# Loading the first tile by partitions instead of by tokens in a weighted combine of expert outputs

## The chip, the cores and the metric

The kernel runs on one core of one Trainium2 chip. The metric is the device time of one execution in microseconds (us); lower is better. Most executions of a kernel agree within 0.3%.

## The reference

For every one of 16 x 1024 = 16,384 tokens there are k = 2 expert outputs of 512 float32 numbers each and two weights. The result is the weighted sum of the two.

```python
batch, seq, hidden, n_experts, k = 16, 1024, 512, 8, 2
expert_outputs: [batch, seq, k, hidden] float32      # 67.1 MB
combine_weights: [batch, seq, k] float32

weights = combine_weights[..., np.newaxis]
return np.sum(expert_outputs * weights, axis=2).astype(np.float32)   # 33.6 MB
```

## The kernel before

Each of the 128 partitions of the on-chip memory takes 128 tokens. A token is one row of 4 KB in the input (two experts of 2 KB) and 2 KB in the output. The tokens of one partition lie one behind the other in HBM, so that a partition's part of a load is one contiguous run: 13 tokens are 52 KB. (The last 13 tokens of every partition come from a second region of the input, which changes nothing in this.)

The work is cut into ten tiles of 12 or 13 tokens per partition, all 128 partitions wide (`TILES`). One tensor `et` holds four rooms, `ROOM = [13, 13, 12, 13]`, and tile g uses room g mod 4. Per tile:

- A load from HBM into the room, issued by SyncE (`load`, line 76). Loads go to SyncE's DMA queue, called q1 in the profile.
- `combine`: for tiles 0 to 7, one VectorE multiplication of the whole room with the broadcast weights (line 88) and one VectorE addition of the two halves (line 97), which writes the sums densely into the front of the room. Tile 8 is shared between ScalarE (line 92) and VectorE (lines 94, 96, 97). Tile 9 goes token by token, ScalarE (line 102) and then VectorE (line 103).
- A store from the room to the output (line 130). Stores of tiles 0 to 6 are issued by ScalarE into its own DMA queue, called q10; tiles 7 and 8 together, and tile 9, are stored by SyncE.

After the store of tile g is issued, SyncE is given the load of tile g + 4, which has to wait until that store has landed, since it overwrites the same room.

The order is written out by hand. Before the loop over tiles, ScalarE's queue takes a small store of zeros (`zt`, 16 rows of 512 B), the weights `wt` of the first 115 tokens of each partition (115 KB, `weights`, line 79) and the remaining weights in two small pieces. SyncE's queue takes the loads of tiles 0 to 3. Tile 0 is loaded in two pieces, 2 tokens and then 11 tokens, the first of them with packets limited to 4 KB. The first multiplication on VectorE needs both pieces and the weights.

A DMA is dealt out over up to 16 DMA engines; each row of a load is one packet on one of them, unless a limit on the packet size cuts it. Both queues are served by the same 16 engines.

Of the kernel before, what the change touches and what calls it, by code (L numbers as in the profile page):

```python
# [1 line left out]

# [4 lines left out]


@with_exitstack
def kernel(  # L10
    ctx: ExitStack,
    tc: tile.TileContext,
    expert_outputs: bass.AP,
    combine_weights: bass.AP,
    out: bass.AP,
):

    nc = tc.nc
    b, s, k, h = expert_outputs.shape
    assert k == 2
    n = b * s
    P = nc.NUM_PARTITIONS
    per = n // P
    assert per * P == n

    ROOM = [13, 13, 12, 13]
    ROOMS = len(ROOM)  # L30
    SITE = [sum(ROOM[:i]) for i in range(ROOMS)]
    TILES = [13, 13, 12, 13, 13, 13, 12, 13, 13, 13]
    FIRST = [2, 11, 13, 12, 13]
    STORES = [[0], [1], [2], [3], [4], [5], [6], [7, 8], [9]]
    WHOLE = [0, 1, 2, 3, 4, 5, 6, 7]
    MIXED = [8]
    ALONE = 3
    FREE = {9: 0}
    LAST = 13
    assert all(c <= ROOM[g % ROOMS] for g, c in enumerate(TILES))  # L40
    assert sum(TILES) == per and [g for st in STORES for g in st] == list(range(len(TILES)))
    main = per - LAST
    starts = [sum(TILES[:g]) for g in range(len(TILES))]

    def rows(x):

        first = x[0 : P * main, :].rearrange("(p t) f -> p t f", p=P)
        second = x[P * main : n, :].rearrange("(p t) f -> p t f", p=P)
        return lambda t, c: first[:, t : t + c, :] if t < main else second[:, t - main : t - main + c, :]

    flat = out.rearrange("b s h -> (b s) h")
    eo = rows(expert_outputs.rearrange("b s k h -> (b s) (k h)"))
    cw = rows(combine_weights.rearrange("b s k -> (b s) k"))
    o = rows(flat)

    dt = mybir.dt.float32
    mult = mybir.AluOpType.mult
    add = mybir.AluOpType.add
    copy = mybir.ActivationFunctionType.Copy

    pool = ctx.enter_context(tc.tile_pool(name="all", bufs=1))
    et = pool.tile([P, sum(ROOM), k * h], dt)
    halves = et.rearrange("p j (k h) -> p (j k) h", k=k)
    wt = pool.tile([P, per * k], dt)
    wk = wt.rearrange("p (t k) -> p t k", k=k)
    zt = pool.tile([16, 128], dt)
    warm = pool.tile([P, 1], dt)

    def place(t):
        g = max(g for g in range(len(TILES)) if starts[g] <= t)  # L70
        return SITE[g % ROOMS] + t - starts[g]

    def load(t, c, **kw):
        at = place(t)
        assert place(t + c - 1) == at + c - 1
        nc.sync.dma_start(out=et[:, at : at + c], in_=eo(t, c), **kw)  # L76

    def weights(q, t, c):
        q.dma_start(out=wk[:, t : t + c, :], in_=cw(t, c))

    def combine(g, base):
        at, c, t0 = SITE[g % ROOMS], TILES[g], starts[g]
        if g in WHOLE or g in MIXED:
            room = halves[:, k * at : k * (at + c), :]
            x0, x1 = et[:, at : at + c, 0:h], et[:, at : at + c, h : 2 * h]
            if g in WHOLE:
                wb = wt[:, k * t0 : k * (t0 + c)].unsqueeze(2).to_broadcast([P, k * c, h])
                nc.vector.tensor_tensor(out=room, in0=room, in1=wb, op=mult)  # L88
            else:
                for i in range(ALONE, c):  # L90
                    x = et[:, at + i, 0:h]
                    nc.scalar.activation(out=x, in_=x, func=copy, scale=wt[:, k * (t0 + i) : k * (t0 + i) + 1])  # L92
                w1 = wk[:, t0 : t0 + c, 1:2].to_broadcast([P, c, h])
                nc.vector.tensor_tensor(out=x1, in0=x1, in1=w1, op=mult)  # L94
                w0 = wk[:, t0 : t0 + ALONE, 0:1].to_broadcast([P, ALONE, h])
                nc.vector.tensor_tensor(out=x0[:, 0:ALONE], in0=x0[:, 0:ALONE], in1=w0, op=mult)  # L96
            nc.vector.tensor_tensor(out=halves[:, base : base + c, :], in0=x0, in1=x1, op=add)  # L97
            return
        for i in range(c):
            t = k * (t0 + i)  # L100
            x0, x1 = halves[:, k * (at + i), :], halves[:, k * (at + i) + 1, :]
            nc.scalar.activation(out=x0, in_=x0, func=copy, scale=wt[:, t : t + 1])  # L102
            nc.vector.scalar_tensor_tensor(  # L103
                out=halves[:, base + i, :], in0=x1, scalar=wt[:, t + 1 : t + 2], in1=x0, op0=mult, op1=add
            )

    with tc.manual_schedule():
        nc.vector.memset(zt, 0.0)  # L108

        ahead = flat[0 : P * main, :].rearrange("(q t) h -> q (t h)", q=16)  # L110
        nc.scalar.dma_start(out=ahead[:, 0:128], in_=zt)  # L111
        weights(nc.scalar, 0, main)
        for half in (slice(0, P // 2), slice(P // 2, P)):
            nc.scalar.dma_start(out=wk[half, main:per, :], in_=cw(main, per - main)[half])
        nc.scalar.activation(out=warm, in_=nc.const_aps.tensor(1.0, (P, 1), dt), func=copy)  # L115

        t = 0
        for i, c in enumerate(FIRST):
            load(t, c, **({"max_dma_last_dim": k * h * 4} if i == 0 else {}))
            t += c  # L120
        assert t == sum(TILES[:ROOMS])
        for j, st in enumerate(STORES):
            room = FREE.get(st[0], st[0] % ROOMS)
            base, c = SITE[room] * k, 0
            for g in st:
                combine(g, base + c)
                c += TILES[g]
            assert c <= k * ROOM[room]
            q = nc.sync if j in (7, 8) else nc.scalar
            q.dma_start(out=o(starts[st[0]], c), in_=halves[:, base : base + c, :])  # L130
            for g in st:
                if g + ROOMS < len(TILES):
                    load(starts[g + ROOMS], TILES[g + ROOMS])


# [1 line left out]
_INS = ['expert_outputs', 'combine_weights']  # L137
_OUTS = [((16, 1024, 512), 'float32')]


# [23 lines left out]
```

## Time and profile before

| What | Value |
|---|---|
| Median time of 3 runs | 238.85 us (238.83 to 238.9) |
| The profiled execution: span, first to last instruction | 237.1 us |
| The profiled execution's own time (taken as the median of the runs, since no other time of it is given) | 238.85 us, so some 1.75 us lie outside the span |
| VectorE (DVE) busy | 190.0 us, 80% of the span |
| ScalarE (ACT) busy | 15.8 us, 7% |
| HBM read, written | 67.24 MB, 33.56 MB |
| Mean rate of all DMA | 425 GB/s |
| Share of the 16 DMA engines: queue q1, queue q10 | 75.9%, 23.0% |

In the profile, DVE is VectorE, ACT is ScalarE, SP is SyncE; "SPq" and "ACTq" are the instruction queues of SyncE and ScalarE, where DMAs are issued and semaphores waited for. L88 is line 88 of the kernel. `et<-in_expert_outputs_dram` is a load, `out_dram<-et` a store. The row of digits after DMA gives the busy share of the DMA engines in 40 equal slices of the span, in tenths, 9 being 90% or more. A row of windows gives the stretch, its length, the busy time of each engine with the number of its instructions, the clock, the DMA share and the rate. DMA packets include completion marks of 4 B, one for each engine that takes part in a DMA. A packet is counted in the stretch in which it starts.

### The profile page before, as it was taken

How to read it: one execution, taken by the hardware profiler on the slowest of the kernel's cores; microseconds unless marked ns; L12 is line 12 of the kernel's file. 1: busy time of each engine (PE TensorE's matmuls, PEld its weight loads, DVE VectorE, ACT ScalarE, POOL GpSimd, SP SyncE). 2: the span in 40 equal slices, each digit the busy share in tenths (PEclk: the TensorE clock that was granted, in tenths of full speed). 3: DMA queues.
4: the chain of work that ended last, by engine and by line, in shares of the span. 5: the costliest groups of instructions: out<-in, count | busy, mean ns of one | idle time of the engine just before them, and what ended most of it. 6: DMA issues, size and time to landing. Idle time of an engine off the chain costs nothing.

```text
span 237.1 us, 154 instructions
## 1 busy us (share of the span) xinstructions
DVE 190.0 (80%) x33; ACT 15.8 (7%) x25; POOL 0.2 (0%) x4
## 2 busy tenths in 40 slices
DVE  0006999999999999999999998998499969919400
ACT  2000000000000000000000000000000055019200
POOL 0000000000000000000000000000000000000000
DMA  8999999989999999999899999999899999899996
GB/s 300 388 481 434 432 421 398 470 348 485 449 431 458 431 440 390 486 420 420 359 492 409 409 509 392 431 503 431 359 431 503 420 397 483 381 431 431 431 431 287
DMA packets 3344, 100.80 MB, mean 425 GB/s; under 512 B 512, under 2 KB 656, under 8 KB 912
## 3 DMA queue, kind: packets, MB, share of 16 engines
q1 hardware_dynamic: 2000, 77.33, 75.9%
q10 hardware_dynamic: 1344, 23.47, 23.0%
HBM read 67.24 MB, written 33.56 MB: 425 GB/s over the span
## 4 chain that ended last, share of the span: by engine, by line
DVE 55%; DMA 36%; issue 1%; ACT 0%; DVEq 0%; ACTq 0%; SPq 0%
DVE et L88 35%; DVE et L97 17%; DMA out_dram<-et 17%; DMA et<-in_expert_outputs_dram 12%; DMA wt<-in_combine_weights_dram 8%; DVE et L103 3%; ACT et L102 0%; DVEq L159 0%; ACTq L111 0%; DVE zt L108 0%; DVEq L88 0%; SPq L76 0%; ACTq L102 0%
## 5 line engine op out<-in xcount | busy, mean ns | idle before, releaser
L88 DVE TENSOR_TENSOR et<-et,wt 128x13312 f32<-128x13312 f32 (+1 forms) x8 | 110.0, 13754 | 23.8 <-DMA wt<-in_combine_weights_dram 18.7
L97 DVE TENSOR_TENSOR et<-et 128x6656 f32<-128x6656 f32 (+1 forms) x9 | 62.8, 6973 | 0.4
L92 ACT ACTIVATE et<-et,wt 128x512 f32<-128x512 f32 x10 | 6.2, 708 | 188.0 <-DMA et<-in_expert_outputs_dram 188.0
L103 DVE SCALAR_TENSOR_TENSOR et<-et,wt 128x512 f32<-128x512 f32 x13 | 8.7, 747 | 5.0 <-ACT et L102 5.0
L102 ACT ACTIVATE et<-et,wt 128x512 f32<-128x512 f32 x13 | 8.1, 707 | 14.0 <-DMA et<-in_expert_outputs_dram 14.0
L94 DVE TENSOR_TENSOR et<-et,wt 128x6656 f32<-128x6656 f32 x1 | 7.1, 7093 | 2.3 <-DMA et<-in_expert_outputs_dram 2.3
L96 DVE TENSOR_TENSOR et<-et,wt 128x1536 f32<-128x1536 f32 x1 | 1.8, 1751 | 0.0
L115 ACT ACT_TABLE_LOAD x1 | 1.3, 1283 | 3.1 <-issue 3.1
L108 DVE MEMSET zt<- 16x128 f32 x1 | 0.2, 165 | 0.8 <-PEq L148 0.8
L115 ACT ACTIVATE warm<-const-float32-1.0 128x1 f32<-128x1 f32 x1 | 0.2, 203 | 0.0
L148 POOL MEMSET const-bfloat16-1.0<- 128x1 bf16 x1 | 0.1, 102 | 0.0
L148 POOL MEMSET const-uint8-127<- 128x1 uint8 x1 | 0.1, 101 | 0.0
L148 POOL MEMSET const-float32-0.0<- 128x1 f32 x1 | 0.1, 99 | 0.2 <-issue 0.2
L148 POOL MEMSET const-float32-1.0<- 128x1 f32 x1 | 0.1, 98 | 0.0
## 6 DMA issues: line engine op xcount, KB each, us to landing
et<-in_expert_outputs_dram SPq DMA_DIRECT2D x7, 6656.0 KB, 32.2
out_dram<-et ACTq DMA_DIRECT2D x5, 3328.0 KB, 34.7
et<-in_expert_outputs_dram SPq DMA_DIRECT2D x2, 6144.0 KB, 41.1
out_dram<-et SPq DMA_DIRECT2D x1, 6656.0 KB, 19.9
out_dram<-et ACTq DMA_DIRECT2D x2, 3072.0 KB, 37.2
et<-in_expert_outputs_dram SPq DMA_DIRECT2D x1, 5632.0 KB, 18.2
out_dram<-et SPq DMA_DIRECT2D x1, 3328.0 KB, 14.0
et<-in_expert_outputs_dram SPq DMA_DIRECT2D x1, 1024.0 KB, 5.0
```

What stands on the lines that cost most here:

```text
L88: nc.vector.tensor_tensor(out=room, in0=room, in1=wb, op=mult)
L92: nc.scalar.activation(out=x, in_=x, func=copy, scale=wt[:, k * (t0 + i) : k * (t0 + i) + 1])
L94: nc.vector.tensor_tensor(out=x1, in0=x1, in1=w1, op=mult)
L96: nc.vector.tensor_tensor(out=x0[:, 0:ALONE], in0=x0[:, 0:ALONE], in1=w0, op=mult)
L97: nc.vector.tensor_tensor(out=halves[:, base : base + c, :], in0=x0, in1=x1, op=add)
L102: nc.scalar.activation(out=x0, in_=x0, func=copy, scale=wt[:, t : t + 1])
L103: nc.vector.scalar_tensor_tensor(out=halves[:, base + i, :], in0=x1, scalar=wt[:, t + 1 : t + 2], in1=x0, op0=mult, op1=add)
L108: nc.vector.memset(zt, 0.0)
L115: nc.scalar.activation(out=warm, in_=nc.const_aps.tensor(1.0, (P, 1), dt), func=copy)
L148: nc = _bacc.Bacc("TRN2", target_bir_lowering=False, num_devices=1)
```

## The change

The first tile is loaded in two pieces again, but cut by partitions: first all 13 tokens of the partitions 0 to 15, then all 13 tokens of the partitions 16 to 127. Each row of both pieces is 52 KB. The limit of 4 KB per packet on the first load goes. All other loads, the weights, the computation and the stores are untouched.

```diff
-    FIRST = [2, 11, 13, 12, 13]
+    FIRST = [13, 13, 12, 13]
+    HEAD = 16
...
-    def load(t, c, **kw):
+    def load(t, c, own=slice(0, P)):
         at = place(t)
         assert place(t + c - 1) == at + c - 1
-        nc.sync.dma_start(out=et[:, at : at + c], in_=eo(t, c), **kw)
+        nc.sync.dma_start(out=et[own, at : at + c], in_=eo(t, c)[own])
...
         for i, c in enumerate(FIRST):
-            load(t, c, **({"max_dma_last_dim": k * h * 4} if i == 0 else {}))
+            for own in (slice(0, HEAD), slice(HEAD, P)) if i == 0 else (slice(0, P),):
+                load(t, c, own)
             t += c
```

## The prediction

> **What bounds the kernel now.** I read the page first, its totals and its row of DMA shares.
>
> ```profile
> span 237.1 us, 154 instructions
> DVE 190.0 (80%) x33; ACT 15.8 (7%) x25; POOL 0.2 (0%) x4
> DMA  8999999989999999999899999999899999899996
> DMA packets 3344, 100.80 MB, mean 425 GB/s; under 512 B 512, under 2 KB 656, under 8 KB 912
> ```
>
> VectorE is busy for 80% of the span, the DMA row shows 9 nearly everywhere. Which of the two sets the end is read from single stretches, so the windows come next (columns: length, busy time of the engines, clock, DMA share, GB/s).
>
> ```profile
> 8.00:20.00 12.00, 0.27 (x1) 0.00 (x0) 0.00 (x0) 1.00 1.02 440
> 100.00:200.00 100.00, 92.53 (x11) 6.23 (x10) 0.00 (x0) 1.00 1.00 435
> ```
>
> The DMA share is full while VectorE does almost nothing (8 to 20 us) and while it works (100 to 200 us), at about the same rate. So the 16 DMA engines are the bound: 100.80 MB at 435 GB/s are 231.7 us of the 237.1. What a change does to the time is then what it adds to or takes from the engines' work, unless it lets them run dry. The 5.4 us that are left lie mostly at the two ends. The front end, from the DMA view of the stretch 0 to 6 us in 40 slices of 0.15 us, and of the stretch 1.8 to 5 us:
>
> ```profile
> GB/s 0 0 0 0 0 0 0 0 0 0 0 0 300 164 82 55 0 191 218 246 355 382 410 437 410 382 413 423 444 413 437 437 437 1256 2758 1202 0 0 0 0
> DMA packets 277, 1.01 MB, mean 315 GB/s; under 512 B 17, under 2 KB 33, under 8 KB 277
> ```
>
> Twelve empty slices: the first byte moves at 1.8 us. Then it takes until about 3 us to reach the full rate. (The high numbers after 4.9 us are an artefact: a packet is counted whole in the slice in which it starts, and the 44 KB ones start there.) In 1.8 to 5 us, 1.01 MB were moved where 3.2 us at 435 GB/s would be 1.39 MB: the ramp costs 0.38 MB, or 0.87 us.
>
> Last I looked for the places where the engines could run dry: the timeline, the issues (size, us from issue to landing) and SyncE's waits.
>
> ```profile
> 0.73 4.52 SPq L76 DMA_DIRECT2D et<-in_expert_outputs_dram  x5
> ...
> 19.73 14.02 DVE L88 TENSOR_TENSOR et<-et,wt 128x13312 f32<-128x13312 f32 x1 [18.75 <-DMA wt<-in_combine_weights_dram]
> ...
> 169.18 14.03 DVE L88 TENSOR_TENSOR et<-et,wt 128x13312 f32<-128x13312 f32 x1 [3.94 <-DMA et<-in_expert_outputs_dram]
> ...
> 208.61 14.02 SPq L130 DMA_DIRECT2D out_dram<-et  x2
> 212.80 8.07 ACT L102 ACTIVATE et<-et,wt 128x512 f32<-128x512 f32 x13 [13.95 <-DMA et<-in_expert_outputs_dram]
> ```
>
> ```profile
> et<-in_expert_outputs_dram SPq DMA_DIRECT2D x7, 6656.0 KB, 32.2
> ...
> out_dram<-et SPq DMA_DIRECT2D x1, 6656.0 KB, 19.9
> et<-in_expert_outputs_dram SPq DMA_DIRECT2D x1, 5632.0 KB, 18.2
> out_dram<-et SPq DMA_DIRECT2D x1, 3328.0 KB, 14.0
> et<-in_expert_outputs_dram SPq DMA_DIRECT2D x1, 1024.0 KB, 5.0
> wt<-in_combine_weights_dram ACTq DMA_DIRECT2D x1, 115.0 KB, 18.2
> ```
>
> ```profile
> SPq L76 <- DMA out_dram<-et: 152.6, 6, 38.4
> ```
>
> A tile of 6,656 KB is 6.82 MB, 15.7 us at 435 GB/s, yet lands 32.2 us after its issue: there is about one more tile's worth of work ahead of it each time, so a load or store that is issued some us later does not empty the queues. At the end the big store is issued at 208.6, the last load lands by 212.8, so the engines have 4.2 us of work left at that moment and need about 1.1 of it (first issue at 0.7, first byte at 1.8). The last store (issued near 222.3, and landed 14.0 us later) finds the big one in flight until 228.5. And VectorE's late multiplications (169.18) wait for loads, not the other way round. So VectorE is off the path by about 3 us at its tightest place.
>
> **The change, part by part.** Removed: a load of 2 tokens in 4 KB packets (1,024 KB) and one of 11 tokens (5,632 KB). Added: a load of rows 0 to 15 and one of rows 16 to 127 of the same tile. Bytes, number of DMA instructions, SyncE's order and the two landings that the first multiplication waits for stay as they were; nothing new is queued behind anything. What changes is how the first 15.7 us of the DMA engines' work are cut.
>
> How is a load of 16 rows dealt out? The trace holds one transfer of 16 rows, the small store of zt. The DMA view of 3.9 to 4.6 us:
>
> ```profile
> DMA packets 103, 0.30 MB, mean 427 GB/s; under 512 B 16, under 2 KB 32, under 8 KB 103
> q10 hardware_dynamic: 32, 0.01, 5.1%
> ```
>
> ScalarE's queue q10 has 32 packets there. The packet line has 16 under 512 B, the completion marks of 16 engines, and 16 more under 2 KB: the rows of 512 B. So 16 rows go one to each engine. Then the first piece is one packet of 52 KB on every engine and the second is 112 / 16 = 7 packets on every engine. In the Trainium skill, "DMA: Bandwidth & Descriptors", section "Why a DMA increments its semaphore by 16 and not by 1", the engines used are the largest number up to 16 that divides the row count; the zt rows agree, and 112 would give 16 too.
>
> Term 1, the ramp. Without the 4 KB packets it may shrink, at most by all of the 0.87 us, at least by nothing (what is late may be the first bytes themselves). I take half: 0.4 us gained.
>
> Term 2, the first piece. A whole tile is 8 rows per engine in 15.7 us, so one row is 1.96 us when all 128 partitions are in play. Every large transfer of this trace is spread over all 128 partitions. The new piece is the first that has 16 engines write into 16 neighbouring partitions, and if neighbours share a way into the memory, the engines wait for each other. Bounds from the rows: nothing shared, 1.96 us; all 16 behind one way, 16 x 1.96 = 31 us. No row is near to either end. I take the middle in ratio, four rows to a way: 4 x 1.96 = 7.8 us, which adds 5.9 us. The Trainium skill, "SBUF — State Buffer", section "Door 1: The DMA port swizzle", speaks against this change: partitions 0 to 15 reach only 4 of 16 ports, measured there at 104 GB/s for 1 MiB. By that, 0.85 MB take 8.2 us; by the trace's nearest row (435 GB/s) 1.96. No run so far shows which holds when each engine has one row.
>
> Term 3, the second piece. Seven rows per engine at 1.96 are 13.7 us if no two engines meet. But if there are 16 ways with 8 rows of the tile each, 12 of them stood idle during the first piece and still have all 8 rows to take: at least 8 x 1.96 = 15.7 us. Upper bound: every row meets another one, 27.4 us. I take 15.7, the bound that follows from the count alone.
>
> What is the path? The DMA engines never idle, each has the same share of all later transfers, and every landing needs its slowest engine; so what the slowest engine loses at the front it still lacks at the end. VectorE's start moves along, and the tail keeps its 3 us of slack. Sum: 7.8 + 15.7 = 23.5 against 15.7 us, +7.8, less 0.4: +7.4 us. The profiled execution has a span of 237.1 us, which with some 1.75 us around it is the median 238.85 of the runs; I add to that: 246.3 us.
>
> **The rivals.** *Nothing is shared (the other side).* If the 27 GB/s of each engine (435 / 16) is the engine's own limit, and not that of the place it writes to, only term 1 is left: 238.85 - 0.4 = 238.4, between 238.0 and 238.85. For it: the same rate in stretches with loads alone (440) and with stores among them (435), so one limit serves both directions. Against it: those stretches all use the whole partition range, so they can't tell the two limits apart. A delay beside it: the 115 KB of weights took 18.2 us to land for 0.3 us of bytes; they go in turns with the large packets, and with turns of 1.96 us rather than 1.7 us may land one turn later. VectorE then starts 2 us later, inside its 3 us of slack: no cost until that is used up. The size of a measurable difference is 0.2%, 0.5 us, so this case is split between faster and same.
>
> *The second piece also jams (slower still).* Seven neighbouring rows per engine start at partitions 16, 23, 30 and so on, with no regard to the ways; two engines then meet again and again. Between 13.7 and 27.4 us the middle is 20.6; 7.8 + 20.6 = 28.4, +12.8 - 0.4: 251.2, at most 258. It decides from the point where the second piece takes over 18 us (248.5).
>
> *A smaller jam.* Two rows to a way, or ways with room for two engines: 3.9 us and then 13.7 to 15.7, so +1.5 to +3.5: 240.4 to 242.3.
>
> *It doesn't do what it says.* 112 rows may be dealt out as 14 engines with 8 rows and two with none: 15.7 us behind an unshared first row of 1.96, +1.96 - 0.4: 240.4, in the same bracket as the smaller jam.
>
> **How the numbers follow.** Four to a way and the second piece near its bound (243 to 248.5): 0.34, the forecast. Second piece jams too (248.5 to 253): 0.26. Nothing shared (238.0 to 239): 0.24. A smaller jam, or 14 engines (239 to 243): 0.10. Worse than 253: 0.06. That sharing is likelier than not is a judgement; no row of before decides it. The likeliest case's own range is 244.3 (only the first piece slow) to 248.5. The range for all is 238.0 to 252.5: cutting it short at either end would drop a case of 0.24 or most of one of 0.26. Faster: 0.14 of the unshared case; same: its other 0.10; slower: the rest, 0.76.
>
> **What would show it.** In the DMA view of the first 10 us, the packets of the second piece start near 4 us (1.8 + 1.96) if nothing is shared, near 9.6 us (1.8 + 7.8) with four to a way. The first multiplication would start near 27 us (19.7 + 7.4) by the forecast, near 32 if the second piece jams, within 18.5 to 21.7 if nothing is shared. The last load should land as much later as the first multiplication starts later; if it doesn't, the claim that the front's loss stays to the end is wrong. Packets: 4 KB ones gone, 16 x 8 of 52 KB in their place. The forecast is wrong if the first 16-row load lands 5 us after its issue or sooner.

## The result and the profile after

The changed kernel takes 255.44 us (median of 5 runs, 255.32 to 256.11), the kernel before 238.85 us beside it: 1.0695 times as long, 95% interval 1.0673 to 1.0717, or 16.6 us more. The forecast was 246.3 us with a range up to 252.5: the way was right, the size was not.

Totals of the changed kernel's page:

```profile
span 253.5 us, 154 instructions
DVE 189.9 (75%) x33; ACT 15.8 (6%) x25; POOL 0.2 (0%) x4
DMA  9799989999999999999999999999999999999995
GB/s 134 153 256 282 265 341 455 395 411 458 469 403 403 428 449 416 470 401 485 401 411 443 430 464 394 445 428 458 462 412 412 428 430 460 447 407 412 470 395 218
DMA packets 3088, 100.80 MB, mean 398 GB/s; under 512 B 512, under 2 KB 656, under 8 KB 656
```

VectorE's busy time (189.9 for 190.0) and the bytes are the same, and the DMA row still shows full engines. But "busy" and "moving bytes" have parted: the first six slices of 6.3 us move 134 to 341 GB/s with engines that show as busy. The windows say it with lengths that compare, after and then before (the last two columns are the DMA share and GB/s):

```profile
0.00:20.00 20.00, 0.17 (x1) 1.49 (x2) 0.20 (x4) 1.00 1.03 210
20.00:40.00 20.00, 1.63 (x1) 0.00 (x0) 0.00 (x0) 1.00 0.94 286
40.00:60.00 20.00, 19.97 (x3) 0.00 (x0) 0.00 (x0) 1.00 0.98 423
```

```profile
0.00:20.00 20.00, 0.44 (x2) 1.49 (x2) 0.20 (x4) 1.00 0.95 390
20.00:40.00 20.00, 19.96 (x2) 0.00 (x0) 0.00 (x0) 1.00 1.00 429
```

Nearly the whole loss lies before 40 us. The DMA views of the first 60 us put a number on it, after and before:

```profile
DMA packets 734, 18.39 MB, mean 307 GB/s; under 512 B 240, under 2 KB 384, under 8 KB 384
```

```profile
DMA packets 1184, 25.17 MB, mean 420 GB/s; under 512 B 256, under 2 KB 400, under 8 KB 656
```

6.78 MB fewer have been started by then, 15.6 us at 435 GB/s, of the 16.4 us by which the span grew. The rest is at the very end, where the last 13.5 us move 323 GB/s instead of 379 (DMA share 0.75 instead of 0.88).

How the front goes, from the DMA view of the first 10 us of the changed kernel (40 slices of 0.25 us, then issues with KB and us to landing):

```profile
GB/s 0 0 0 0 0 0 426 2556 426 0 0 0 0 0 0 0 0 0 0 0 0 0 0 0 0 0 0 0 0 215 0 215 215 215 219 1071 6 1071 213 0
...
et<-in_expert_outputs_dram SPq DMA_DIRECT2D x1, 5824.0 KB, 35.1
et<-in_expert_outputs_dram SPq DMA_DIRECT2D x1, 832.0 KB, 10.2
wt<-in_combine_weights_dram ACTq DMA_DIRECT2D x1, 115.0 KB, 36.8
...
out_dram<-zt ACTq DMA_DIRECT2D x1, 8.0 KB, 10.2
```

All 16 packets of the head start at about 1.8 us; the next ones start between 7.5 and 9.5. By the packet records of the trace (start and length of each packet), the head's 52 KB packets took 5.7 to 7.4 us, 6.9 on average, where such a packet takes 1.97 elsewhere. The second piece, issued at 1.2, lands at 36.3; the weights land 2 us later still. And the timeline from there on:

```profile
38.37 14.02 DVE L89 TENSOR_TENSOR et<-et,wt 128x13312 f32<-128x13312 f32 x1 [37.40 <-DMA wt<-in_combine_weights_dram]
...
184.61 14.03 DVE L89 TENSOR_TENSOR et<-et,wt 128x13312 f32<-128x13312 f32 x1 [1.93 <-DMA et<-in_expert_outputs_dram]
...
224.06 14.94 SPq L132 DMA_DIRECT2D out_dram<-et  x2
229.17 8.07 ACT L103 ACTIVATE et<-et,wt 128x512 f32<-128x512 f32 x13 [14.87 <-DMA et<-in_expert_outputs_dram]
```

The first multiplication starts 18.6 us later than before, the big store is issued 15.5 later, the last load lands 16.4 later: what the front loses reaches the end nearly whole, and 2.2 us of VectorE's later start are taken up by its slack.

### The profile page after: what moved, and what is told of

It is laid out like the page before. It is cut to its first block, busy times and chain, and to the rows that moved or that the text cites. A ratio compares the mean times of both kernels' runs of the same rounds, so it can differ in the third digit from the quotient of the medians.

```text
span 253.5 us, 154 instructions
## 1 busy us (share of the span) xinstructions
DVE 189.9 (75%) x33; ACT 15.8 (6%) x25; POOL 0.2 (0%) x4
## 4 chain that ended last, share of the span: by engine, by line
DVE 49%; DMA 40%; issue 4%; ACT 0%; DVEq 0%; ACTq 0%; SPq 0%
DVE et L89 33%; DMA out_dram<-et 15%; DMA wt<-in_combine_weights_dram 15%; DVE et L98 13%; DMA et<-in_expert_outputs_dram 11%; DVE et L104 3%; ACT et L103 0%; DVEq L161 0%; ACTq L112 0%; DVE zt L109 0%; DVEq L89 0%; SPq L77 0%; ACTq L103 0%
## 6 DMA issues: line engine op xcount, KB each, us to landing
out_dram<-et ACTq DMA_DIRECT2D x2, 3072.0 KB, 37.6
out_dram<-et SPq DMA_DIRECT2D x1, 3328.0 KB, 14.1
et<-in_expert_outputs_dram SPq DMA_DIRECT2D x1, 832.0 KB, 10.2
```

## The experiments

The theory (W): the 128 partitions are reached over ways that each carry the rate of one DMA engine, 27 GB/s, and engines that write over the same way at the same time share it. Rivals: the reads meet in HBM, any load of fewer rows is slow, or the late weights do it.

**Which places are slow.** Four lone loads ahead of the kernel before, each waiting for the last:

```diff
+        x = expert_outputs.rearrange("b s k h -> (b s) (k h)")
+        nc.sync.dma_start(out=et[0:16, 0:13], in_=eo(0, 13)[0:16])
+        nc.sync.dma_start(out=et[0:121:8, 0:12], in_=eo(0, 12)[0:121:8])
+        nc.sync.dma_start(out=et[0:106:7, 0:11], in_=eo(0, 11)[0:106:7])
+        nc.sync.dma_start(out=et[0:16, 0:10], in_=x[0:160, :].rearrange("(p t) f -> p t f", p=16))
```

> The kernel before, with four extra loads ahead of it, one after the other, each waiting for the one before and all overwritten by the tile's own load: 16 rows each, (1) partitions 0 to 15, 13 tokens; (2) every eighth partition, 12 tokens; (3) every seventh partition from 0 to 105, 11 tokens; (4) partitions 0 to 15 again, 10 tokens, but from one contiguous stretch of HBM. A load alone is taken as 2 us plus its transfer. Theory W: (1) four to a way, 4 x 1.97 + 2 = 9.9 us; (2) two to a way, 2 x 1.82 + 2 = 5.6; (3) twelve engines alone and two pairs, 2 x 1.67 + 2 = 5.3; (4) as the first by size, 4 x 1.52 + 2 = 8.1. Rival S (the reads meet in HBM, since neighbouring rows lie 471 KB apart): (4) is quick, 3.5 us. Rival C (16 rows are slow anywhere): (2) and (3) as slow as (1) by size, 9.1 and 8.4 us.

Its issues (KB, us to landing), in the order of the diff:

```profile
et<-in_expert_outputs_dram SPq DMA_DIRECT2D x1, 832.0 KB, 10.0
et<-in_expert_outputs_dram SPq DMA_DIRECT2D x1, 768.0 KB, 6.5
et<-in_expert_outputs_dram SPq DMA_DIRECT2D x1, 704.0 KB, 5.6
et<-in_expert_outputs_dram SPq DMA_DIRECT2D x1, 640.0 KB, 8.2
```

10.0, 6.5, 5.6 and 8.2 against W's 9.9, 5.6, 5.3 and 8.1; the second is 0.9 us over. The same 16 rows' worth is quick when spread, so the row count is not it; the last one reads one contiguous stretch of HBM and is as slow as neighbours are, so HBM is not it. The destination is. The time of the run (268.99 us) is about 238.9 plus the 30.3 us that the four took.

**How many rows.** The same with 64, 112, 112 and 128 rows:

```diff
+        nc.sync.dma_start(out=et[0:64, 0:13], in_=eo(0, 13)[0:64])
+        nc.sync.dma_start(out=et[0:112, 0:12], in_=eo(0, 12)[0:112])
+        nc.sync.dma_start(out=et[16:128, 0:11], in_=eo(0, 11)[16:128])
+        nc.sync.dma_start(out=et[:, 0:10], in_=eo(0, 10))
```

> The kernel before, with four extra loads ahead of it, one after the other as in the run with the four places: (1) partitions 0 to 63, 13 tokens; (2) partitions 0 to 111, 12 tokens; (3) partitions 16 to 127, 11 tokens; (4) all 128, 10 tokens. Theory W: (1) four rows of 2 x 1.97 us + 2 = 17.7 us; (2), (3) seven neighbouring rows per engine that meet others most of the time, as the second piece did (about 3.5 us a row of 13 tokens): 24.6 and 22.7 us; (4) 8 x 1.52 + 2 = 14.1. Rival D (the second piece was slow only because it came behind the disorder of the first): (2) 14.7 and (3) 13.7 us. Rival H (only one row per engine is slow): (1) 9.9 us.

```profile
et<-in_expert_outputs_dram SPq DMA_DIRECT2D x1, 5376.0 KB, 24.2
et<-in_expert_outputs_dram SPq DMA_DIRECT2D x1, 5120.0 KB, 14.6
et<-in_expert_outputs_dram SPq DMA_DIRECT2D x1, 4928.0 KB, 24.1
et<-in_expert_outputs_dram SPq DMA_DIRECT2D x1, 3328.0 KB, 19.5
```

The lines are sorted by size: 64 rows 19.5 us, 112 rows 24.2 and 24.1, 128 rows 14.6. W had 17.7, 24.6, 22.7 and 14.1, but its price of a row among 112 was read off the changed kernel's second piece and not worked out from meetings. A load of 112 rows is slow by itself, with no head before it (D falls). Less 2.3 us for a lone load, the one of partitions 16 to 127 takes 21.8 us for seven rows of 44 KB per engine, 3.1 us a row. A row of 44 KB alone would be 1.66 (52 KB in 1.96): 1.87 times as long.

The packet records of this run show more. The packets of each load of 112 rows, put in order of their starts and taken by sixteens (one row for each engine), have these median lengths in us:

| Load | 1st row | 2nd | 3rd | 4th | 5th | 6th | 7th | such a packet undisturbed |
|---|---|---|---|---|---|---|---|---|
| partitions 16 to 127, 44 KB | 3.14 | 3.21 | 2.52 | 2.40 | 3.01 | 3.21 | 2.98 | 1.67 |
| partitions 0 to 111, 48 KB | 3.28 | 3.40 | 3.45 | 2.38 | 2.43 | 3.28 | 3.43 | 1.82 |

Suppose that each engine has seven neighbouring rows, and that a way serves four neighbours and the four that lie 32 further (the pairs below bear this out). Counting then gives two pairs of engines that meet in each row, but only one pair in the 3rd and 4th row of the first load and in the 4th and 5th row of the second. Those are the short rows, which speaks for seven neighbours to an engine. But all sixteen engines are slow: in the 2nd row of the first load no packet took less than 3.18 us, though by this count twelve engines meet nobody and would need 1.67. A meeting thus seems to hold up the engines that don't meet as well. W does not say that, and no run here shows why. (The HBM side was not varied for 112 rows; but with seven neighbours to an engine the sources lie equally far apart in each of the seven rows, so HBM alone would not explain the short ones.)

**Cut in halves.** `HEAD = 64` in the changed kernel.

> The first tile cut at partition 64 instead of 16: rows 0 to 63, then rows 64 to 127. Theory W, with four neighbouring rows for each engine and 32 partitions between two that share a way: both pieces have two engines to a way all the time, 8 rows of 3.93 us = 31.5 us instead of 15.7, so 238.85 + 15.7 - 0.4 = 254.2 us. The Trainium skill, SBUF - State Buffer, Door 1: partitions 0 to 63 reach 8 of 16 ports. Rival H (only a head with one row per engine is slow): the head's four rows per engine spread, under 243 us. Rival C (every load with fewer than 128 rows is slow by its row count): about as slow as the 16/112 cut, 252 to 258 us, which this run alone does not tell from W.

255.80 us, ratio 1.0710 (1.0692 to 1.0728), for 254.2 expected. The DMA view from 8 to 32 us:

```profile
DMA packets 224, 5.20 MB, mean 217 GB/s; under 512 B 32, under 2 KB 128, under 8 KB 128
```

217 GB/s is half of 435: two engines to a way, in both halves. The Trainium skill, "SBUF — State Buffer", "Door 1: The DMA port swizzle", gives 8 of 16 ports for partitions 0 to 63 and about 218 GB/s as the limit for large transfers; this run agrees.

**The head in short packets.** The limit of 4 KB put back on the head (`load` passes the keyword on to `dma_start`; those lines are left out here):

```diff
-                load(t, c, own)
+                load(t, c, own, **({"max_dma_last_dim": k * h * 4} if own.stop == HEAD else {}))
```

> The cut at 16 partitions, with the head in packets of 4 KB again. Theory W: the head's bytes share four ways whatever the packets are, so the front loses the same: 253 to 256 us. ScalarE's queue gets short turns again, so the weights land well ahead of the 36.8 us after their issue that the changed kernel needs; the first multiplication then waits for the second piece, near 37 us. Rival L (most of the loss is the late landing of the weights behind 52 KB packets): the weights land early and the time falls below 250 us.

255.77 us, ratio 1.0693 (1.0648 to 1.0739). W's time holds. The DMA view from 3 to 7 us, and issues of this run:

```profile
DMA packets 121, 0.50 MB, mean 124 GB/s; under 512 B 0, under 2 KB 0, under 8 KB 121
```

```profile
et<-in_expert_outputs_dram SPq DMA_DIRECT2D x1, 832.0 KB, 10.6
wt<-in_combine_weights_dram ACTq DMA_DIRECT2D x1, 115.0 KB, 37.6
out_dram<-zt ACTq DMA_DIRECT2D x1, 8.0 KB, 10.6
```

124 GB/s where a spread load has 435: 3.5 times less, the same as with the 52 KB packets (6.9 us for 1.97). W's four engines that share the rate of one would make it 4 times; no run here shows where the difference comes from. The expectation for the weights was wrong: they landed no earlier (37.6), for the zeros ahead of them in their queue landed only with the head (10.6), and after that the turns were long ones again.

**Which partitions share.** First a mixed row of lone loads and stores; it also gave the direction of stores.

```diff
+        nc.sync.dma_start(out=et[0:8, 0:13], in_=eo(0, 13)[0:8])
+        nc.sync.dma_start(out=et[0:29:4, 0:12], in_=eo(0, 12)[0:29:4])
+        nc.sync.dma_start(out=et[0:65:64, 0:11], in_=eo(0, 11)[0:65:64])
+        nc.sync.dma_start(out=et[0:33:32, 0:10], in_=eo(0, 10)[0:33:32])
+        nc.sync.dma_start(out=et[:, 0:9], in_=eo(0, 9))
+        nc.sync.dma_start(out=o(0, 16)[0:16], in_=halves[0:16, 0:16, :])
+        nc.sync.dma_start(out=o(0, 18)[0:121:8], in_=halves[0:121:8, 0:18, :])
```

> The kernel before, with lone transfers ahead of it, each waiting for the one before, all overwritten later. A lone one is taken as 2.3 us plus its transfer. Loads: (1) partitions 0 to 7, 13 tokens; (2) every fourth partition from 0 to 28, 12 tokens; (3) partitions 0 and 64, 11 tokens; (4) partitions 0 and 32, 10 tokens; (5) all 128, 9 tokens. Stores: (6) partitions 0 to 15, 32 KB each; (7) every eighth partition, 36 KB each. Theory W with four neighbours to a way and the partition 32 further on the same way (the Trainium skill, SBUF - State Buffer, Door 1, states this layout): (1) 4 x 1.97 + 2.3 = 10.2; (2) 4.1; (3) 4.0; (4) 2 x 1.51 + 2.3 = 5.3; (5) 13.2. Rival N (neighbourhood alone counts): (4) 3.8. If reads of the memory share the ways as writes do: (6) 4 x 1.21 + 2.3 = 7.1 and (7) 2 x 1.36 + 2.3 = 5.0; if not, 3.5 and 3.7.

SyncE's timeline; each issue waits for the landing before it, so the differences of the first column are the times:

```profile
0.72 0.40 SPq L117 DMA_DIRECT2D et<-in_expert_outputs_dram  x1
10.11 0.79 SPq L118 DMA_DIRECT2D et<-in_expert_outputs_dram  x1
14.71 0.50 SPq L119 DMA_DIRECT2D et<-in_expert_outputs_dram  x1
18.88 0.47 SPq L120 DMA_DIRECT2D et<-in_expert_outputs_dram  x1
23.73 0.37 SPq L121 DMA_DIRECT2D et<-in_expert_outputs_dram  x1
37.24 0.35 SPq L122 DMA_DIRECT2D out_dram<-et  x1
43.67 0.58 SPq L123 DMA_DIRECT2D out_dram<-et  x1
48.23 2.68 SPq L76 DMA_DIRECT2D et<-in_expert_outputs_dram  x5
```

9.4, 4.6, 4.2, 4.9, 13.5, 6.4 and 4.6 us. Eight neighbours are slow, eight at distance four are not. The fourth (partitions 0 and 32) came out between W's 5.3 and N's 3.8, so it decides nothing. The stores: 32 KB rows from neighbours take 6.4 us, 36 KB rows from spread partitions 4.6, so stores, which read the memory, jam as well. (Their places in HBM were not varied, so here the HBM side is not excluded.)

To settle partition 32, pairs with three loads in a row, so that two engines write without a break:

```diff
+        def two(s, r):
+            return {"out": et[0 : s + 1 : s, SITE[r] : SITE[r] + 13], "in_": eo(13 * r, 13)[0 : s + 1 : s]}
+
+        for r in (0, 1, 3):
+            nc.sync.dma_start(**two(64, r))
+        for r in (3, 1, 0):
+            nc.sync.dma_start(**two(32, r))
+        for r in (0, 1, 3):
+            nc.sync.dma_start(**two(4, r))
+        for r in (3, 1, 0):
+            nc.sync.dma_start(**two(1, r))
```

> The kernel before, with four groups of extra loads ahead of it, each of three loads of two partitions (52 KB to each, three rooms one behind the other, so two engines write 156 KB each without a break); a group begins when the one before has landed. Partitions 0 and 64, then 0 and 32, then 0 and 4, then 0 and 1. A group whose two engines don't meet takes 3 x 1.97 + 2.3 = 8.2 us, one whose engines share a way 3 x 3.93 + 2.3 = 14.1 us. Theory W with four neighbours to a way and the partition 32 further on the same way: 8.2, 14.1, 8.2, 14.1. Rival N (neighbours alone): 8.2, 8.2, 8.2, 14.1. If only many engines at once jam, and never two: 8.2 for all four.

```profile
0.73 1.70 SPq L121 DMA_DIRECT2D et<-in_expert_outputs_dram  x3
9.31 1.58 SPq L123 DMA_DIRECT2D et<-in_expert_outputs_dram  x3
23.64 1.91 SPq L125 DMA_DIRECT2D et<-in_expert_outputs_dram  x3
32.18 0.88 SPq L127 DMA_DIRECT2D et<-in_expert_outputs_dram  x3
45.73 2.67 SPq L76 DMA_DIRECT2D et<-in_expert_outputs_dram  x5
```

8.6, 14.3, 8.5 and 13.6 us: 0 and 64 don't meet, 0 and 32 do, 0 and 4 don't, 0 and 1 do. That is W's pattern and not that of either rival. It agrees with the layout that the Trainium skill gives on the page named above: four neighbours on a port, and those 32 further on the same one.

**The other half of the change, and the weights.** The limit alone taken off the kernel before, the first tile in one load, and the same with weights that don't have to wait:

```diff
# no limit (on the kernel before)
-            load(t, c, **({"max_dma_last_dim": k * h * 4} if i == 0 else {}))
+            load(t, c)
# whole tile (on the changed kernel)
-            for own in (slice(0, HEAD), slice(HEAD, P)) if i == 0 else (slice(0, P),):
+            for own in (slice(0, P),):
# weights first (on the whole tile, on the changed kernel, on the kernel before)
-        weights(nc.scalar, 0, main)
+        weights(nc.sync, 0, main)
```

No limit:

> The kernel before (2 tokens, then 11, all partitions) without the limit of 4 KB on the first load: its packets are 8 KB. This is the other half of the change done alone. Theory: the turns are still short at the front, so the zeros and the weights are served as before and the first multiplication starts at 19.5 to 20 us; 238.4 to 239.2 us. Rival (the 4 KB limit itself is what the whole-tile run lost): 240 us or more.

238.87 us, ratio 0.9998 (0.9989 to 1.0007): no difference.

The whole tile in one load:

> The first tile in one load of all 128 partitions, 52 KB rows, no cut and no limit on the packet size. Theory W (16 DMA engines that write into partitions of the same way into the memory share the rate of one engine, 27 GB/s): a 128-row load has no such meeting, so only the ramp changes: 238.0 to 238.85 us, first multiplication at 19 to 20 us. Rival F (large packets are slow at the very front, whatever partitions they write to): well over 243 us.

242.52 us, ratio 1.0151 (1.0136 to 1.0166): neither. From its timeline and its page:

```profile
25.74 14.03 DVE L89 TENSOR_TENSOR et<-et,wt 128x13312 f32<-128x13312 f32 x1 [24.76 <-DMA wt<-in_combine_weights_dram]
```

```profile
wt<-in_combine_weights_dram ACTq DMA_DIRECT2D x1, 115.0 KB, 24.2
```

The first multiplication waited 6.0 us longer than before, and for the weights. Two runs on that, the whole tile in 4 KB packets (the limit on this one load) and the weights ahead of it:

> The first tile in one load of all partitions, all of it in 4 KB packets. Theory T: the weights get short turns, land within 8 us, and the first multiplication waits for the tile at 20 to 21 us; a 4 KB packet takes a little longer by the byte than a large one (the ramp's rows of before), so 239 to 240 us. Rival (one load instead of two for the first tile costs the time): 242 us.

239.86 us, ratio 1.0035 (1.0017 to 1.0053), as expected. Issue and timeline:

```profile
wt<-in_combine_weights_dram ACTq DMA_DIRECT2D x1, 115.0 KB, 6.8
```

```profile
20.76 14.03 DVE L89 TENSOR_TENSOR et<-et,wt 128x13312 f32<-128x13312 f32 x1 [19.78 <-DMA et<-in_expert_outputs_dram]
```

> The first tile in one load of all partitions, as in the run with the whole tile (242.5 us), but the weights of the first 115 tokens are issued by SyncE ahead of the loads instead of by ScalarE. Theory T (the whole tile's +3.6 us comes from the weights: each packet of theirs waits for a turn of a 52 KB packet, so they land at 25.6 us and not 19.6, and VectorE's start uses up its slack of about 3 us): first multiplication at 19 to 20.5 us and 238.3 to 239.3 us. Rival F (the large first packets themselves cost it): 242 us with an early first multiplication.

240.70 us (239.3 to 241.07), ratio 1.0055 (1.0031 to 1.0080), with the first multiplication at 19.84 in the profiled execution: half of the loss is gone, less than expected. The kernel before with the same edit says why:

> The kernel before, with the weights of the first 115 tokens issued by SyncE ahead of the loads. The engines are busy from 1.8 us on as before and the first multiplication waits for the tile instead of the weights, at 19.3 to 19.8 us: 238.5 to 239.1 us, no measurable gain, since VectorE's start is not on the path. Rival: the start of VectorE is on the path and the time falls with it, by up to 0.5 us.

240.63 us (239.25 to 241.26), ratio 1.0059 (1.0039 to 1.0080), the first multiplication at 19.73. Putting the weights first costs 1.7 us by itself, which neither theory expected and which stays open: the two profiled executions took 239.30 and 239.59 us, less than their medians, so their traces don't show the whole cost. With the weights first, the whole tile in one load and the two loads by tokens are equal (240.70 and 240.63), so large packets at the front cost nothing but the turns that the other queue waits for. How the late weights turn into 3.6 us (3.1 in the profiled execution) is shown in part by the packet records. The first multiplication and with it the first store are 6 us later, so the load of the fifth tile, which waits for that store's room, is issued at 75.72 us instead of 67.80. From 74.1 to 79.5 us no load moves, only stores. The packets of loads that start between 79.5 and 92 us take up to 3.2 us instead of 1.97, which costs some 1.1 us, and the last 13.5 us move 323 GB/s instead of 379, some 1.7 us. Why the packets are longer there is not shown.

And the changed kernel with the weights first:

> The changed kernel (cut at 16 partitions), but the weights of the first 115 tokens are issued by SyncE ahead of the loads. The first multiplication then waits for the second piece alone, near 36.5 us instead of 38.4. Theory W (the DMA engines' time lost in the two pieces is the loss; the later start of VectorE is covered by its slack): 254.7 to 256.1 us, as the changed kernel. Rival L (the 2 us by which the weights come after the tile are part of the loss): 252.5 to 254 us.

256.05 us, ratio 1.0706 (1.0683 to 1.0729); the first multiplication starts at 37.46 and waits for the tile. VectorE starts 0.9 us earlier than in the changed kernel and nothing is gained, as W has it; L's 252.5 to 254 is not met. But weights first cost the kernel before 1.7 us. If it costs as much here, 255.44 + 1.7 - 256.05 = 1.1 us of the loss can still belong to the late weights. So L is not ruled out for a part of that size; the other 15 us or more do not depend on the weights.

## Why the prediction was wrong in size

**The bound and the path** were right: the DMA engines' time at the front is carried to the end (of the 16.4 us by which the span grew, 15.6 are seen before 60 us), and VectorE's slack was put at 3 us and took up 2.2. That the weights might land a turn of the queue later, behind the tile, was right too; it cost 1.1 us at most, by the last run above.

**Term 2, the head,** was nearly right: 7.8 us taken and 6.9 measured on average, its successors foreseen near 9.6 us and found between 7.5 and 9.5, and a landing 10.2 us after issue. The value was only the middle between two bounds, so that it came so close is luck; now the jam of the head is shown (10.0 us lone, 124 GB/s in short packets), at 3.5 times and not 4.

**Term 3, the second piece, is the step that failed.** It was taken at 15.7 us, the bound from the count of rows, with 20.6 as a rival and 27.4 as the end. Scaled to 13 tokens, the lone load of 112 rows takes 21.8 x 13 / 11 = 25.8 us; in the changed kernel itself it is 25.7 us from the end of the head's last packet (9.4) to the end of the second piece's last (35.2). With that the sum is 7.8 + 25.8 - 15.7 = +17.9, less the 0.4 of term 1 +17.5, against +16.6 measured. The rest is in the 15.7 that the sum takes off: by the packet records the first tile of the kernel before is moved from 1.8 to 18.9 us, in 17.1 us, and that of the changed kernel ends 16.3 us later. So the mechanism of the rival "the second piece also jams" came true, but it too was sized too small: its 20.6 us, the middle between its bounds, gave 251.2 and a share of 0.26 up to 253, while the measured 255.44 lies where the prediction had put 0.06. The fault in reasoning: the lower bound counts rows per way, as if sixteen engines would always stand before sixteen different ways. Seven neighbours per engine make them meet by turns, and that was written in the rival and not in the term. The size comes from a second thing that neither had: where two pairs at most meet by count, all sixteen engines take 1.9 times as long (3.21 us for 1.67). The runs show the jam of 112 rows; that the seven are neighbours fits the short rows of both loads, and why engines that don't meet are slow stays open.

**Term 1, the ramp,** was taken as 0.4 us gained; without the limit alone the gain is nil (238.87). Its 8 KB packets have moved 0.14 MB more by 5 us, 0.3 us of work, but nothing of that is left at the end. With 52 KB packets (the whole tile) no more has been moved by 5 or 20 us than before, and the other queue's turns are longer.

**The rival "nothing is shared"** (0.24) fell with the pairs of partitions. The equal rate of loads and stores, quoted for it, spoke for both: stores from neighbours jam too.

## What to carry to other kernels

On this chip a load or store of a part of the partitions is not that part of a whole one: with one tile cut by partitions, this kernel took about 17 us longer than with the tile cut by tokens, and 13 us longer than with it whole, where each piece uses all 128 partitions. If fewer partitions have to move, spread them. Measured quick were partitions four apart (a pair, and eight of them from 0 to 28) and 64 apart, slow those one apart and 32 apart. In a profile, look at GB/s beside the busy share: engines that wait for each other look busy.

## What the runs showed of the hardware that was not expected

- Two engines alone on one way take about twice as long: three 52 KB packets in 13.6 to 14.3 us less 2.3, 3.8 to 4.0 us each, against 1.97 alone. But in a load of 112 rows all sixteen engines are slow at once, also those that by count meet nobody (3.18 us or more for 1.67).
- Two queues take turns by packet, and a packet is as long as a row: the same 115 KB of weights landed after 6.8 us beside 4 KB packets, 24.2 us beside 52 KB ones.
- 115 KB of weights issued ahead of the loads, landed by 3 us, made the kernel before 1.7 us slower, with runs between 239.25 and 241.26 us. No run here says why.
